# Where the last dots of the modulation weights run in a hybrid attention and convolution layer

## The chip, the cores and the metric

The kernel runs on one core of a Trainium2 chip. The metric is the device time of one execution in microseconds (us). The engines are TensorE (PE; PEld is its weight load), VectorE (DVE), ScalarE (ACT), GpSimd (POOL) and SyncE (SP), which issues all DMA transfers here from one queue in order.

## The reference

One layer over x (1024 tokens x 1024) with a context of 256 tokens. All six modulation vectors come from one product with `w_ada`; for the context the first two of them are needed.

```
sh1, sc1, gt1, sh2, sc2, gt2 = split(silu(c) @ w_ada + b_ada, 6)
csh1, csc1, ... = split(silu(c_ctx) @ w_ada + b_ada, 6)
hc = rmsnorm(ctx, g_pre_mix) * (1 + csc1) + csh1
kc, vc, gates_f, gates_b = parts of hc @ w_in         # gates: log_sigmoid(a @ w + b) / 16
s_f, s_b = final states of a gated linear attention over the context, both directions
hx = rmsnorm(x, g_pre_mix) * (1 + sc1) + sh1
p = hx @ w_in                                          # k, v, gates, q, og, sb, sc, sx
o = chunked gated linear attention from s_f and s_b, both directions, rmsnorm, * silu(og)
o_sc = sb * row_convolution(sc * sx)
x = x + gt1 * rmsnorm(concat(o, o_sc) @ w_out, g_post_mix)
x = x + gt2 * rmsnorm(conv_ffn(rmsnorm(x, g_pre_ffn) * (1 + sc2) + sh2), g_post_ffn)
```

## The kernel before

Products run on PE in three passes over values split in a high and a low part (`mm3`, whose lines L145 to L147 carry most of PE's records). Tokens go in tiles of 128: eight of x (`NT`) and two of the context (`NCT`).

The modulation vectors aren't made on PE. Of each 128 columns of `w_ada` a tile of 128x1024 floats (512 KB) is loaded, and DVE multiplies it by the broadcast silu(c) and sums along the row (L230, a "dot"). The first 16 are done early. The other 48 are drawn from one list by `some_ada(n)`: it first does the dots of all pending loads, then issues n new loads. In the text below they are numbered 0 to 47: loads 0 to 15 are of the context's shift and scale, 16 to 47 are columns 16 to 47, for gt1, sh2, sc2, gt2. Unless a place is given, a load goes by turns, `nada % 3`, into the pools `px` ("x"), `pgt` ("ada") and `px` again: loads with number 1, 4, ..., 19, 22, ..., 40, 43, 46 go to the one buffer of `ada`, the rest to `x`, which has eight buffers that `bc`, `gc`, `kw`, `kc`, `vc`, `hch`, `hcl`, `mraw`, `su` use as well. A load waits until its buffer has been read.

The stages around the change, in PE's order, which is the written one throughout:

- the q and token-major steps of x and the context. `token_major(2, tk)` for eight tiles of x, with loads 4 to 19; the context's keys `kc` for two tiles; `token_major(2, ...)` for the two tiles of the context; then `token_major(1, tk)` for eight tiles of x ("token steps", loads 20 to 37, three in the first two steps and two in the others), and for the two tiles of the context ("context steps", no loads).
- `gla()` and `stream()`, which take turns. `gla` first makes the gates: `ctx_decay(j)` for the two context tiles, then `decay(c)` for eight tiles c. Each is a product on PE (`gates_psum`, L486) into one of two banks, three steps on ACT (tile `ge`) and one on DVE (L495, result `gc` or `g`), which frees the bank. `ctx_keys` and `sums(c)` (L757: cumulative sums of g on PE, read by ACT into `bc`) follow one and two steps behind; `kx_prep` (L775 and L778 on DVE, an exponential on ACT) needs `bc`; `kx_turn` and `update` follow. `stream` is the rest of the input projection, 24 matrix products at a time for a half block, with the row convolution (L691 to L701 on DVE).
- In `gla` the ten last loads (38 to 47) are issued one a step, all into the buffer of `ada`, each done in the step behind it; `masks` (for the attention levels much later) are cast at c = 0 from `mraw`.

DVE, ACT and POOL keep the written order inside the token-major block, DVE also inside the first two steps of `gla` (`ORDERED`); there are two such blocks one behind the other, not tied to each other. Everything else on DVE, ACT, POOL and SP is put in order at build time by a planner from its own costs, with the program's order as priority; it may put an instruction ahead of others that are written earlier. So `row<-gv` (L1041, 1024 floats written to DRAM one by one, from gt1) is issued long before the place where it stands.

Of the kernel before, what the change touches and what calls it, by code (L numbers as in the profile page):

```python
# [8 lines left out]
F32 = mybir.dt.float32  # L9
# [12 lines left out]
P = 128  # L22
KT = D // P
NT = T // P
NCT = CT // P
H = 4
DK = 64
# [92 lines left out]
def build(nc, ap, out, dbg=None):  # L120
    V, S, G, PE, SY = nc.vector, nc.scalar, nc.gpsimd, nc.tensor, nc.sync
    names = iter(range(10**9))

    def nm(s="t"):
        return f"{s}{next(names)}"

    def act(o, i, fn=AF.Copy, **kw):
        return S.activation(o, i, fn, **kw)  # L128
# [13 lines left out]
    def mm3(ps, lhs, rhs, first, last, more=False):  # L142

        (lh, ll), (rh, rl) = lhs, rhs
        PE.matmul(ps, lh, rh, start=first, stop=False, skip_group_check=more)  # L145
        PE.matmul(ps, lh, rl, start=False, stop=False, skip_group_check=more)  # L146
        PE.matmul(ps, ll, rh, start=False, stop=last, skip_group_check=more)  # L147

    with tile.TileContext(nc) as tc, tc.manual_schedule(engines={mybir.EngineType.PE}):
        pools = {}  # L150

        def popen(name, side=None, **kw):
            cm = tc.tile_pool(name=name, side=side, **kw)
            pools[name] = (cm, cm.__enter__())
            return pools[name][1]
# [19 lines left out]
        def bank(n):  # L175
            return pools[n][1].tile([P, 512], F32, tag=n, name=nm("ps"))
# [30 lines left out]
        px = popen("px", "right", bufs=8)  # L207
        pgt = popen("pgt", "left", bufs=1)
# [12 lines left out]
        def ada_load(j, pool, tag, bufs):  # L221
            raw = pool.tile([P, D], F32, tag=tag, bufs=bufs, name=nm("ada"))
            SY.dma_start(raw, ap["ada"][j])
            return raw

        def ada_dot(j, which, raw, eng=None):

            dst = (gcol, gctx)[which][:, j : j + 1]
            if eng is None:
                V.tensor_tensor_reduce(raw, raw, cbs[which], 1.0, 0.0, ALU.mult, ALU.add, dst)  # L230
            else:
                eng.tensor_tensor(raw, raw, cbs[which], ALU.mult)
                act(raw, raw, AF.Copy, accum_out=dst)
# [265 lines left out]
        def ctx_load():  # L499
            for j in range(NCT):  # L500
                cxs.append(x_load(ap["ctx"], j))
                cdg.append(rms_diag(cxs[j]))
# [22 lines left out]
        def hc(kt, j):  # L525
            s = slice(j * P, (j + 1) * P)
            return hch[kt // 4][:, kt % 4, s], hcl[kt // 4][:, kt % 4, s]

        def token_major(g, tk, lhs, vv):
            pp = bank(ps_mm)  # L530
            for kt in range(KT):
                mm3(pp[:, :272], lhs(kt), (wah[g, kt], wal[g, kt]), kt == 0, kt == KT - 1)
            if g == 1:
                act(vv[:, :272], pp[:, :272])
                return
            al = cp.tile([P, 32], F32, tag="al", bufs=3, name=nm("al"))
            act(al, pp[:, 240:272])
            act(vv[:, 272:], pp[:, :240])
            als[tk] = al
# [9 lines left out]
        def xlhs(tk):  # L549
            s = slice(tk * P, (tk + 1) * P)  # L550
            return lambda kt: (hxh[kt][:, s], hxl[kt][:, s])
# [5 lines left out]
        def some_ada(n, where=None):  # L557

            for a, raw in pend:
                ada_dot(a[0], a[1], raw, a[2])  # L560
            pend.clear()
            for _ in range(n):
                a = next(adas, None)
                if a is not None:
                    where_ = where or ((px, "x", 8), (pgt, "ada", 1), (px, "x", 8))[nada[0] % 3]
                    pend.append((a, ada_load(a[0], *where_)))
                    nada[0] += 1

        als = {}
        with tc.manual_schedule(engines={mybir.EngineType.Activation, mybir.EngineType.DVE, mybir.EngineType.Pool}):  # L570
            ctx_load()
            some_ada(4)
            for hf in range(2):
                pq1 = bank(ps_mm)
                tsl = slice(hf * 512, hf * 512 + 512)
                for kt in range(KT):
                    mm3(pq1, wq1[kt], (hxh[kt][:, tsl], hxl[kt][:, tsl]), kt == 0, kt == KT - 1)
                act(qh[hf][:, 1, :], pq1, AF.Copy, scale=DK ** -0.5)
            for t in range(NT):
                vt[t] = pvo.tile([P, VW], F32, tag="vo", name=nm("v"))  # L580
            for tk in range(NT):
                some_ada(3 if tk < 3 else 2 if tk < 5 else 1)
                if tk == 3:
                    ada_affine_ctx(0)
                if tk == 5:
                    ada_affine_ctx(4)
                if 4 <= tk < 8:
                    ctx_lo()
                token_major(2, tk, xlhs(tk), vt[tk])
                if tk > 1:  # L590
                    put_aT(tk - 2)
                if 3 <= tk < 7:
                    ctx_lo = ctx_norm(tk - 3)
                if tk == NT - 1:
                    for kt in range(4):
                        wa_load(1, kt)
                        wa_split(1, kt)
            put_aT(NT - 2)
            kc = px.tile([P, NCT, QK], F32, tag="x", name="kc")
            vc = px.tile([P, NCT, VW], F32, tag="x", name="vc")  # L600
            for j in range(NCT):
                pp = bank(ps_mm)
                for kt in range(KT):
                    mm3(pp[:, :QK], hc(kt, j), (wah[0, kt][:, :QK], wal[0, kt][:, :QK]), kt == 0, kt == KT - 1)
                act(kc[:, j, :], pp[:, :QK])
            put_aT(NT - 1)
            for kt in range(4, KT):
                wa_load(1, kt)
            for j in range(NCT):
                token_major(2, NT + j, lambda kt: hc(kt, j), vc[:, j, :])  # L610
            for kt in range(4, KT):
                wa_split(1, kt)
            for tk in range(NT):
                some_ada(3 if tk < 2 else 2)
                token_major(1, tk, xlhs(tk), vt[tk])
                if 0 < tk <= NCT:
                    put_aT(NT + tk - 1)
            for j in range(NCT):
                token_major(1, NT + j, lambda kt: hc(kt, j), vc[:, j, :])
        pclose("pst")  # L620

# [1 line left out]
        pg_ = popen("pg", "right", bufs=1)  # L623
        tc.keep_in_program_order(S.preload_act_table_set("natural_log_exp_and_others"))
        masks = pg_.tile([P, 6, DK], U8, name="masks")
        mraw = px.tile([P, 6, DK], F32, tag="x", name="mraw")
        SY.dma_start(mraw, ap["masks"])
        og_d = [dr.tile([4, P, H, P], F32, name=f"ogd{c}") for c in range(2)]
        sc_d = [dr.tile([4, P, H, P], F32, name=f"scd{c}") for c in range(2)]
        x1_d = [dr.tile([P, D], F32, name=f"x1d{c}") for c in range(NT)]  # L630
# [103 lines left out]
        pe_ = popen("pe_", "right", bufs=1)  # L734
        flat = lambda t: t.rearrange("p f t -> p (f t)")

        def gla():
# [29 lines left out]
            def kx_prep(hf, d):  # L767
                e = (P - 1) if d == 0 else 0
                for hh in range(2):
                    act(decv[d * DK : d * DK + DK, hh, :, 4 * hf : 4 * hf + 4],  # L770
                        bc[hf][d][hh * DK : hh * DK + DK].rearrange("p f (c t) -> p f c t", t=P)[:, :, :, e],
                        AF.Exp, scale=ITAU)
                kx = pe_.tile([P, 2, 512], F32, tag="e", bufs=4, name=nm("kx"))
                b3 = bc[hf][d].rearrange("p f (c t) -> p (f c) t", t=P)
                V.tensor_tensor(kx.rearrange("p f (c t) -> p (f c) t", t=P),  # L775
                                b3[:, :, e : e + 1].broadcast_to([P, 8, P]), b3, ALU.subtract)
                act(kx, kx, AF.Exp, scale=ITAU)
                V.tensor_tensor(kx, kx, kh[hf], ALU.mult)  # L778
                kxs[hf, d] = kx
# [47 lines left out]
                V.tensor_copy(slot(NT - 1)[DK:P, :], s0[DK:P, :])  # L827

            slot = lambda c: su[c // 2][:, c % 2, :]
            for j in range(NCT):  # L830
                ctx_decay(j)
                some_ada(1, (pgt, "ada", 1))
                yield 1
            for c in range(NT):
                decay(c)
                if c == 0:
                    V.tensor_copy(masks, mraw)
                if 0 < c <= NCT:
                    ctx_keys(c - 1)
                if c > 1:  # L840
                    sums(c - 2)
                some_ada(1, (pgt, "ada", 1))
                if c == 4:
                    su = [px.tile([P, 2, 512], F32, tag="x", name=f"su{i}") for i in range(4)]
                    ctx_state()
                if c >= NT - 2:
                    kx_prep(0, c - NT + 2)
                yield 0.8 if c > 1 else 1
            some_ada(0)
            sums(NT - 2)  # L850
            yield 0.8
            sums(NT - 1)
# [818 lines left out]
```

## Time and profile before

| what | value |
|---|---|
| three runs | 1153.4, 1157.13 (median), 1157.71 us |
| the profiled execution | 1157.1 us |
| its span, first to last instruction | 1155.3 us |
| PE busy | 1120.4 us, 97% |
| DVE, ACT, POOL busy | 872.3, 528.9, 498.9 us |
| mean granted clock of TensorE | 0.993 |

Times in the profile count from the span's start. A timeline row gives start and duration, engine, line, operation, the tiles written and read, and in brackets how long the engine had been idle and what ended it. A waits row gives who waited for whom: total us, times, longest. The token and context steps of `token_major(1, ...)` run on PE from about 118 to 148 us, the steps of `gla` behind them.

### The profile page before, as it was taken

Reading aid. Unit: us, or ns where it says so; the run is one execution under the profiler, and the core shown is the slowest. Engines: PE = TensorE matmul, PEld = TensorE weight load, DVE = VectorE, ACT = ScalarE, POOL = GpSimd, SP = SyncE. Lnnn points to the kernel's source line nnn. Section 1 sums busy time; section 2 is a strip of 40 time slices with the busy share of each in tenths; the row PEclk is TensorE's granted clock in tenths of the full one; section 3 lists DMA queues with packets and bytes.
Section 4 is the critical chain, followed back from the end, with each engine's and each line's share of the span. In section 5 each row is a group of like instructions: output and inputs, shape, how many; then the busy total and the mean of one; then the engine's idle time right before and its main releaser. Section 6 shows DMA issues by size and latency. Waiting matters only on the chain. (4 is left out here: it accounts for less than half of the span.)

```text
span 1155.3 us, 16916 instructions
## 1 busy us (share of the span) xinstructions
PE 1120.4 (97%) x6272; PEld 927.1 (80%) x6272; DVE 872.3 (76%) x1182; ACT 528.9 (46%) x957; POOL 498.9 (43%) x467
## 2 busy tenths in 40 slices
PE   8899988999999999999999999999999999999997
PEld 6689977888887878887878788888887888888885
DVE  5876657899778556576888978787878787777676
ACT  6845156644344456655233242433333345544443
POOL 5211012347466111128777868687767780000002
PEclk9999999999999999999999999999999999999999
DMA  9884853522113283232343323232323169978572
GB/s 345 311 277 137 275 143 119 149 63 60 46 44 102 59 280 113 79 110 73 91 146 110 109 92 119 92 110 92 119 91 110 66 208 338 357 250 273 195 245 100
DMA packets 80132, 176.00 MB, mean 152 GB/s; under 512 B 9807, under 2 KB 21711, under 8 KB 80050
## 3 DMA queue, kind: packets, MB, share of 16 engines
q1 hardware_dynamic: 80050, 174.93, 45.9%
q8 instruction: 49, 0.80, 0.3%
q14 instruction: 33, 0.27, 0.1%
HBM read 142.12 MB, written 32.78 MB: 151 GB/s over the span
## 5 line engine op out<-in xcount | busy, mean ns | idle before, releaser
L1343 DVE SCALAR_TENSOR_TENSOR y<-u,cols,y 128x945 f32<-128x945 f32 (+2 forms) x176 | 214.8, 1222 | 3.7 <-ACT y L128 1.3
L145 PE MATMUL ps<-mx,p 128*128 128x512 f32 x440 | 174.3, 396 | 4.1 <-DVE g L1398 2.2
L146 PE MATMUL ps<-mx,p 128*128 128x512 f32 x440 | 173.1, 394 | 0.0
L147 PE MATMUL ps<-mx,p 128*128 128x512 f32 x440 | 173.1, 393 | 0.0
L135 POOL TENSOR_TENSOR p<-rs,p 128x512 fp32r<-128x512 f32 x88 | 115.3, 1314 | 88.3 <-ACT p L128 84.5
L643 POOL TENSOR_TENSOR wl<-wr,wh 128x256 fp32r<-128x256 f32 x64 | 62.0, 998 | 158.9 <-ACT wh L128 158.7
L147 PE MATMUL ps<-p,p 128*128 128x512 f32 x308 | 120.1, 390 | 0.2
L146 PE MATMUL ps<-p,p 128*128 128x512 f32 x308 | 120.0, 390 | 0.0
L145 PE MATMUL ps<-p,p 128*128 128x512 f32 x308 | 119.9, 389 | 0.0
L145 PE MATMUL ps<-hxh,wh 128*128 128x512 f32 x256 | 104.5, 408 | 1.2 <-DVE sc L701 1.2
L145 PEld LDWEIGHTS ps<-mx,p 128*128 128x128 f32 x440 | 83.1, 189 | 27.0 <-ACT u L128 5.7
L230 DVE CUSTOM_DVE_ANT_0 ada<-ada,cb 128x1024 f32<-128x1024 f32 x64 | 80.3, 1265 | 31.3 <-DMA ada<-in_ada 30.7
L146 PE MATMUL ps<-hxl,wh 128*128 128x512 f32 x256 | 100.6, 393 | 0.0
L147 PE MATMUL ps<-hxh,wl 128*128 128x512 f32 x256 | 100.5, 393 | 0.0
L128 ACT ACTIVATE p<-rs 128x512 fp32r<-128x512 f32 x88 | 54.5, 623 | 100.5 <-POOL rs L1193 100.5
L147 PEld LDWEIGHTS ps<-mx,p 128*128 128x128 f32 x440 | 83.1, 189 | 18.6
L146 PEld LDWEIGHTS ps<-mx,p 128*128 128x128 f32 x440 | 83.0, 189 | 18.1
L135 POOL TENSOR_TENSOR p<-wr,p 128x512 fp32r<-128x512 f32 x58 | 76.1, 1312 | 13.0 <-ACT p L128 13.0
L128 ACT ACTIVATE y<-u,cols 128x1024 f32<-128x1024 f32 x22 | 26.6, 1210 | 107.1 <-DVE u L1405 107.1
L145 PE MATMUL ps<-b,p 128*128 128x512 f32 x176 | 69.5, 395 | 0.0
L146 PE MATMUL ps<-b,p 128*128 128x512 f32 x176 | 69.4, 394 | 0.0
L147 PE MATMUL ps<-b,p 128*128 128x512 f32 x176 | 69.4, 394 | 0.0
(277 smaller groups left out, 2598.9 us busy)
## 6 DMA issues: line engine op xcount, KB each, us to landing
ada<-in_ada SPq DMA_DIRECT2D x64, 512.0 KB, 4.6
wr<-in_wu SPq DMA_DIRECT2D x48, 512.0 KB, 4.0
h<-hd SPq DMA_DIRECT2D x77, 256.0 KB, 4.5
hd<-h SPq DMA_DIRECT2D x73, 256.0 KB, 2.2
wdr<-in_wd SPq DMA_DIRECT2D x55, 256.0 KB, 3.7
wdr<-in_wd SPq DMA_DIRECT2D x22, 512.0 KB, 5.9
x<-in_x SPq DMA_DIRECT2D x16, 512.0 KB, 4.4
wr<-in_wb SPq DMA_DIRECT2D x16, 512.0 KB, 3.7
```

The source lines that it names most:

```text
L128: return S.activation(o, i, fn, **kw)
L135: (eng or V).tensor_tensor(lo, raw, hi.bitcast(F32), ALU.subtract)
L145: PE.matmul(ps, lh, rh, start=first, stop=False, skip_group_check=more)
L146: PE.matmul(ps, lh, rl, start=False, stop=False, skip_group_check=more)
L147: PE.matmul(ps, ll, rh, start=False, stop=last, skip_group_check=more)
L230: V.tensor_tensor_reduce(raw, raw, cbs[which], 1.0, 0.0, ALU.mult, ALU.add, dst)
L643: eng.tensor_tensor(lo[:, k : k + 2], raw[:, k : k + 2], hi[:, k : k + 2].bitcast(F32), ALU.subtract)
L1343: V.scalar_tensor_tensor(y3[:, ro, co], u3[:, ri, ci], col("wcf", 9 * p + 3 * (dr_ + 1) + dc + 1), y3[:, ro, co], ALU.mult, ALU.add)
```

## The change

- `some_ada(2)` is called in the first step of `kc` (dot 19, loads 20 and 21) and in each of the two context steps. Loads 22 to 39 are issued in the token steps, 40 to 43 in the context steps, and dots 38 to 41 are written in the context steps.
- In `gla` the calls with a place of their own go. There are three calls with two loads each or none left: at j = 1 (dots 42 and 43, loads 44 and 45), at c = 1 (dots 44 and 45, loads 46 and 47) and at c = 3 (dots 46 and 47). The loads take the places by turns.
- `mraw` takes a buffer of the pool `pe_` instead of `px` and is issued inside `gla`; the cast of `masks` stands at c = 2 instead of c = 0.
- `kx_prep(0, 0)` and `kx_prep(0, 1)` stand at c = 5 and 6 instead of 6 and 7.

```diff
             for j in range(NCT):
                 pp = bank(ps_mm)
+                if j == 0:
+                    some_ada(2)
                 for kt in range(KT):
@@
             for j in range(NCT):
+                some_ada(2)
                 token_major(1, NT + j, lambda kt: hc(kt, j), vc[:, j, :])
@@
         masks = pg_.tile([P, 6, DK], U8, name="masks")
-        mraw = px.tile([P, 6, DK], F32, tag="x", name="mraw")
-        SY.dma_start(mraw, ap["masks"])
@@
             slot = lambda c: su[c // 2][:, c % 2, :]
+            mraw = pe_.tile([P, 6, DK], F32, tag="e", bufs=4, name="mraw")
+            SY.dma_start(mraw, ap["masks"])
             for j in range(NCT):
                 ctx_decay(j)
-                some_ada(1, (pgt, "ada", 1))
+                if j:
+                    some_ada(2)
                 yield 1
             for c in range(NT):
                 decay(c)
-                if c == 0:
+                if c == 2:
                     V.tensor_copy(masks, mraw)
                 if 0 < c <= NCT:
                     ctx_keys(c - 1)
                 if c > 1:
                     sums(c - 2)
-                some_ada(1, (pgt, "ada", 1))
+                if c in (1, 3):
+                    some_ada(2)
                 if c == 4:
                     su = [px.tile([P, 2, 512], F32, tag="x", name=f"su{i}") for i in range(4)]
                     ctx_state()
-                if c >= NT - 2:
-                    kx_prep(0, c - NT + 2)
+                if c in (5, 6):
+                    kx_prep(0, c - 5)
                 yield 0.8 if c > 1 else 1
-            some_ada(0)
             sums(NT - 2)
```

## Rows read from the trace of the kernel before

**Rows 1.** The page's busy line of all engines: busy us, share of span, instructions.
```profile
PE 1120.4 (97%) x6272; PEld 927.1 (80%) x6272; DVE 872.3 (76%) x1182; ACT 528.9 (46%) x957; POOL 498.9 (43%) x467
```

**Rows 2.** Waits of PE, 148 to 232 us: us in total, times, longest.
```profile
PE ps L757 <- DVE g L495: 4.7, 2, 4.1
PE ps L486 <- DVE gc L495: 2.4, 1, 2.4
PE ps L486 <- DVE g L495: 1.7, 2, 1.4
PE ps L794 <- ACT kxt L128: 0.2, 1, 0.2
```

**Rows 3.** Timeline of PE, 154 to 200 us: its rows with idle time before them.
```profile
156.84 0.79 PE L486 MATMUL ps<-wgh,aT 98*128 98x512 f32 x1 [2.35 <-DVE gc L495]
...
168.63 0.50 PE L486 MATMUL ps<-wgh,aT 98*128 98x512 f32 x1 [0.31 <-DVE g L495]
...
174.19 0.50 PE L486 MATMUL ps<-wgh,aT 98*128 98x512 f32 x1 [1.38 <-DVE g L495]
...
189.70 1.13 PE L757 MATMUL ps<-tri,g 128*128 128x128 f32 x8 [0.66 <-DVE g L495]
...
197.64 2.00 PE L757 MATMUL ps<-tri,g 128*128 128x128 f32 x8 [4.08 <-DVE g L495]
```

**Rows 4.** Windows: length, busy us by engine, then PEclk, DMA share, GB/s.
```profile
156.70:160.10 3.40, 3.27 (x8) 2.59 (x9) 2.52 (x6) 2.44 (x5) 0.00 (x0) 0.50 0.00 0
...
197.70:201.10 3.40, 3.40 (x14) 3.25 (x15) 1.58 (x2) 1.39 (x6) 0.00 (x0) 0.50 0.75 294
```

**Rows 5.** Timeline of DVE, 151 to 168 us: dots 35 and 38, cast, first gate.
```profile
151.20 1.22 DVE L230 CUSTOM_DVE_ANT_0 ada<-ada,cb 128x1024 f32<-128x1024 f32 x1 [0.15 <-DMA ada<-in_ada]
...
155.82 0.36 DVE L837 CAST masks<-mraw 128x384 uint8<-128x384 f32 x1 [3.39 <-DMA mraw<-in_masks]
156.09 0.69 DVE L495 SCALAR_TENSOR_TENSOR gc<-ps,ge 128x512 f32<-128x512 f32 x1
...
166.73 1.23 DVE L230 CUSTOM_DVE_ANT_0 ada<-ada,cb 128x1024 f32<-128x1024 f32 x1 [5.49 <-DMA ada<-in_ada]
```

**Rows 6.** Timeline of ACT, 151 to 160 us: third step of the first gate.
```profile
152.91 0.73 ACT L128 ACTIVATE ge<-ge,small 128x512 f32<-128x512 f32 x1
```

**Rows 7.** Timeline of SP's queue, 150 to 154 us.
```profile
152.46 0.33 SPq L627 DMA_DIRECT2D mraw<-in_masks  x1
152.84 0.43 SPq L1041 DMA_DIRECT2D row<-gv  x1
```

**Rows 8.** Timeline of DVE, 182 to 198 us: two dots and the last gate.
```profile
182.05 1.23 DVE L230 CUSTOM_DVE_ANT_0 ada<-ada,cb 128x1024 f32<-128x1024 f32 x1 [2.17 <-DMA ada<-in_ada]
...
192.33 1.77 DVE L230 CUSTOM_DVE_ANT_0 ada<-ada,cb 128x1024 f32<-128x1024 f32 x1
...
196.81 0.68 DVE L495 SCALAR_TENSOR_TENSOR g<-ps,ge 128x512 f32<-128x512 f32 x1
```

**Rows 9.** Timeline of DVE, 118 to 146 us: weight splits, dots 20, 23, 32.
```profile
118.99 1.59 DVE L135 TENSOR_TENSOR wal<-war,wah 128x272 fp32r<-128x272 f32 x4 [5.83 <-ACT wah L128]
...
122.39 1.23 DVE L230 CUSTOM_DVE_ANT_0 ada<-ada,cb 128x1024 f32<-128x1024 f32 x1 [0.67 <-DMA ada<-in_ada]
...
128.63 1.23 DVE L230 CUSTOM_DVE_ANT_0 ada<-ada,cb 128x1024 f32<-128x1024 f32 x1 [0.65 <-DMA ada<-in_ada]
...
145.09 1.23 DVE L230 CUSTOM_DVE_ANT_0 ada<-ada,cb 128x1024 f32<-128x1024 f32 x1 [0.21 <-DMA ada<-in_ada]
```

**Rows 10.** The loads of ada issued from 117 to 153 us, time to landing.
```profile
DMA to landing us min/median/max: 3.6/4.3/5.5
```

**Rows 11.** Instructions on the tile kx: ns min/median/max, first and last start.
```profile
L775 DVE TENSOR_TENSOR kx<-bc x4: 1215/1220/1221, 189.5 to 203.7; 128x1024 f32<-128x1024 f32 x4
```

**Rows 12.** All 64 loads of ada in the span, time to landing.
```profile
DMA to landing us min/median/max: 3.3/4.6/9.6
```

**Rows 13.** DMA traffic from 155.7 to 162.3 us.
```profile
DMA packets 0, 0.00 MB, mean 0 GB/s; under 512 B 0, under 2 KB 0, under 8 KB 0
```

## The prediction, made before the change was run

> **What bounds the kernel now.** I read the page's busy line first: TensorE (PE) works 97% of the span, so 35 us of idle PE time and the time at a lowered clock are all that a reordering can win [rows 1]. Then the waits of PE alone, for 148 to 232 us, where the moved dots lie: all but 0.2 us of them end at a `logdecay` result (L495) on VectorE (DVE), in PE's `gates_psum` (L486, which needs the bank that an earlier L495 has read) or in `sums` (L757) [rows 2]. In order of time they are five: 2.35 us before 156.84, 0.31 before 168.63, 1.38 before 174.19, 0.66 before 189.70, 4.08 before 197.64 [rows 3]; together 8.78 us. Next the granted clock: 0.50 in 156.70 to 160.10 and in 197.70 to 201.10, right behind the two long idle times, at the level of 1.2 GHz instead of 2.4. PE was busy for 3.27 and 3.40 us in these, so half of that, 1.6 and 1.7 us, is what the clock took [rows 4]. The stretch thus holds 8.8 + 3.3 = 12.1 us.
>
> Why DVE was late is seen in its own order of time. Before 156.84 it finished dot 35 at 152.43 and stood 3.39 us until `mraw` landed, cast `masks` at 155.82, and only then did `gc` of context tile 0, whose input had been ready since ScalarE's third step ended at 153.64 [rows 5, 6]. `mraw` had been issued at 152.46, right behind dot 35, whose buffer it took [rows 7]. The 0.31 and 1.38 stand behind dots 38 and 39 waiting for their loads: dot 38 waited 5.49 us [rows 5]. The 4.08 is `decay(7)`, done on DVE only at 196.81; in the 15 us before it DVE ran three dots, of 1.23, 1.23 and 1.77 us (the first and the last are shown), the first after 2.17 us of waiting [rows 8].
>
> **The change, part by part.** No dot, load or other instruction is added or lost; only places and buffers change. Loads are numbered 0 to 47 as in the list above.
>
> *Loads 20 and 21 and dot 19 at the kc step.* Dot 19 takes 1.22 us of a stretch in which DVE stood idle for 5.83 us until 118.99, when the `wa` splits began [rows 9]. On SP the two loads pass the `wa` and `wr` loads that follow; what passes is two transfers, some 4.3 us each [rows 10] and one beside the other, of work whose first reader is that split. I cost this at nothing; without the idle time it would be 1.2 us of DVE, ahead of no PE work that waits.
>
> *The token steps.* Three buffers serve the loads: two of `x` and the one of `ada`, since `hch`, `hcl`, `kc` and `vc` hold the other six. Each load waits until the dot three back has freed its buffer, so the stretch is paced by landing plus dot: the loads landed in 3.6 to 5.5 us, median 4.3 [rows 10], and a dot takes 1.22. Before, dot 20 began at 122.39 [rows 9] and dot 35 at 151.20 [rows 5]: 15 dots in 28.8 us, 1.92 us each. The change does not add a buffer. Dots 20 and 21 now run at 120.5 and 121.8, behind the same weight splits (118.99 and 1.59 [rows 9]); load 22 has landed by then, load 23 goes out when dot 20 ends, 121.75, and dot 23 starts 4.3 later, at about 126.0. From there the pace holds.
>
> *The context steps.* Six loads and four dots more than before (dots 38 to 41) are now written ahead of `gc` of tile 0. Dot 41 starts at 126.0 + 18 x 1.92 = 160.6 at the mean pace and at 158.9 at 1.83 us, the pace of the evenest nine (dot 23 at 128.63, dot 32 at 145.09 [rows 9]); it ends 1.2 us later, and `gc`, 0.69, at 160.8 to 162.5. PE stands ready from 154.49 (156.84 less 2.35). So the first stall would not go with the mask cast: it would be 6.3 to 8.0 us instead of 2.35. The bound below is no stall, from `gc` being ready at 153.64. I take 161.0, a stall of 6.55 and so **+4.2 us**, near the lower of the paced values, because `hch` and `hcl` are read for the last time when the token steps end and some of the last loads may get their buffers. Behind that stall the clock falls as it did behind the shorter one; I take 1.7 for 1.6, **+0.1**. Queued behind dots 40 and 41 is all of DVE's first work on the gates, and PE waits for that.
>
> A rule that bears on this: the Trainium skill, "DMA: Bandwidth & Descriptors", section "Anatomy of one DMA", fits a transfer as 2.0 us plus its bytes over 436 GB/s, measured for DMAs issued by GpSimd. That would be 3.2 us for these 512 KB, a pace of 1.5 us and dot 41 ending near 153: no stall, as an estimate by that page. The rows, with 4.3 at the median, do not agree, and I go by them.
>
> *The mask cast.* `mraw` no longer waits for a dot's buffer; its place in SP's queue, with some loads ahead, decides when it lands. The 3.39 us wait is no longer what ends last before `gc`: the dots are. If the planner still puts the cast ahead of `gc`, it costs its 0.36 us, at most until a load issued beside it lands. Taken as nothing, with 1 us as the upper bound.
>
> *Dots 42 to 47, two loads ahead.* Instead of twelve dots in the `gla` steps there are six. The three dots in the 15 us ahead of `decay(7)` go: 1.23 + 1.23 + 1.77 us and 2.17 us of waiting, 6.4 us of DVE's queue, against a stall of 4.08 [rows 8, 3]. I take all of it, **-4.1**, with the clock behind it, **-1.7**, and the 1.38 before 174.19, **-1.4**. I leave 0.31 and 0.66 standing. Bounds: nothing more than 2 us is won if ScalarE's and DVE's `kx` work takes the place, and 8.1 if all four stalls go. The four dots behind 200 us go too, which is worth nothing: in the rest of the stretch PE is kept waiting for 0.2 us [rows 2].
>
> *`kx_prep` one step sooner.* The same instructions, but those of the second direction now stand ahead of `decay(7)`. DVE's two `kx` steps, 1.22 us the first [rows 11] and the second, of the same size, alike, take 2.4 us for one direction; that is less than the 6.4 us freed. Taken as nothing; if they fall just ahead of `decay(7)` up to 2.4 us of the 4.1 come back.
>
> *The sum:* +4.2 + 0.1 - 4.1 - 1.7 - 1.4 = -2.9 us against the profiled execution's 1157.1 us (its span is 1155.3, 1.8 us lie around it; the median of the runs is 1157.13): 1154.2. PE is the bound for the rest, so what is won by 230 us is kept.
>
> **The rivals.** By 0.5%, about what a measurement of this kernel can tell from no change, the bounds are 1151.3 and 1162.9.
>
> *The dots slip behind `gc`.* The two written blocks are not tied to each other, so the planner may place `gc` of tile 0 ahead of dots 40 and 41 if it thinks those loads late. Then the first stall is 2.4 to 4.4 us, as before or a little more, and the rest is won: 1157.1 - 7.2 + 0.6 = 1150.5 (1149 to 1152). For it: the cast was put ahead of `gc` in just this way [rows 5]. Against: the cast came early, so the planner takes loads to be quick, and then the dots come first.
>
> *The loads keep up.* The shortest landing of any load is 3.3 us [rows 12]. If all were so, the pace would be (3.3 + 1.2) / 3 = 1.5 us and dot 41, at 125.05 + 18 x 1.5 = 152.1, would end before `gc` is ready; the stall and its clock loss vanish: 1157.1 - 7.2 - 2.35 - 1.6 = 1145.9. Against it: the pace over 15 dots was 1.92. The page cited above would have it this way.
>
> *The slow row write.* Before, `row<-gv`, 1024 elements of 4 bytes, stood in SP's queue behind `mraw` [rows 7]. Issued at 152.84, it left the DMA engines without a packet from 155.7 to 162.3 [rows 13], and load 38, issued behind it, landed only at 166.7 [rows 5]. If the planner puts that write ahead of load 41, dot 41 and all PE work behind `gc` come up to 9.6 us later (152.84 to about 162.4): 1163.8, slower. It decides from that one place in SP's order; behind load 41 it delays only loads 46 and 47, which have some microseconds.
>
> **How the numbers follow.** Forecast 0.50 (1150 to 1158), dots behind `gc` 0.25, loads keep up 0.13, row write 0.12. The range is to leave out some 0.2: from 1147.0, short of most of the third case, to 1160.0, short of the fourth, and it takes in the bounds of the first stall (from as before to 8.0 us). Faster by over 0.5%: 0.05 of the forecast, 0.15 of the second, all 0.13 of the third: 0.33. Slower: the 0.12. The same: 0.55.
>
> **What would show it.** Right: before the third L486 behind the token steps, PE idle for 5 to 8 us, DVE there in dots that wait for loads, the cast no longer in the way; then no idle of over 1.5 us before 200 us, and one lowered clock instead of two. Wrong, to the faster side: `gc` on DVE right at 154 to 155. Wrong, to the slower: `row<-gv` in SP's queue among loads 38 to 41, or the idle of 4 us before `sums(7)` still there with `kx` in its place.

## The result, and the profile after

The changed kernel took 1159.34 us (median of 22 runs, 1157.03 to 1163.63), the kernel before 1157.72 on the same chip (22 runs): a ratio of means of 1.0019, 95% interval 1.0011 to 1.0028. The time is inside the forecast range and within 0.5%, but on the other side: some 2 us slower, where 2.9 us less were forecast. The profiled execution of the changed kernel took 1158.04 us, with a span of 1155.9. One of the 22 runs of the kernel before took 1379.23 us and is left out of the ratio.

The page's busy line hardly differs [rows 1]:

```profile
PE 1118.3 (97%) x6272; PEld 924.6 (80%) x6272; DVE 870.2 (75%) x1182; ACT 529.0 (46%) x957; POOL 493.0 (43%) x467
```

The waits of PE in the same stretch, 148 to 232 us (total, times, longest), to be held against [rows 2]:

```profile
PE ps L486 <- DVE gc L495: 9.0, 1, 9.0
PE ps L758 <- DVE g L495: 2.3, 1, 2.3
PE ps L486 <- DVE g L495: 0.4, 1, 0.4
PE ps L758 <- ACT kw L128: 0.3, 1, 0.3
```

and in order of time, PE's rows with idle time before them (against [rows 3]):

```profile
162.91 0.79 PE L486 MATMUL ps<-wgh,aT 98*128 98x512 f32 x1 [9.03 <-DVE gc L495]
...
175.61 1.16 PE L758 MATMUL ps<-tri,g 128*128 128x128 f32 x8 [0.35 <-ACT kw L128]
...
179.89 0.50 PE L486 MATMUL ps<-wgh,aT 98*128 98x512 f32 x1 [0.35 <-DVE g L495]
...
200.67 1.13 PE L758 MATMUL ps<-tri,g 128*128 128x128 f32 x8 [2.26 <-DVE g L495]
```

One wait grew from 2.35 to 9.03 us, the last fell only from 4.08 to 2.26, and the three short ones (2.35 in sum) became two of 0.35. The sum went from 8.78 to 11.99 us. The granted clock fell behind the same two waits as before [rows 4]; windows of these two stretches (length, busy us by engine, PEclk, DMA share, GB/s):

```profile
157.39:167.63 10.24, 4.72 (x11) 3.75 (x12) 6.20 (x13) 2.45 (x4) 0.00 (x0) 0.50 0.81 270
...
201.77:205.18 3.41, 3.41 (x12) 2.84 (x11) 2.41 (x3) 3.19 (x10) 0.00 (x0) 0.50 0.59 174
```

Half of PE's busy time in each is what 1.2 GHz instead of 2.4 took: 2.36 and 1.70 us, where it was 1.6 and 1.7. The stretch so holds 11.99 + 4.06 = 16.05 us that could be won, and held 12.1 before: 4.0 more.

Why the first wait is 9 us is in DVE's own order of time (its timeline, dots 23, 24 and 41 and the first gate):

```profile
124.67 1.23 DVE L230 CUSTOM_DVE_ANT_0 ada<-ada,cb 128x1024 f32<-128x1024 f32 x1 [1.30 <-DMA ada<-in_ada]
...
127.23 1.23 DVE L230 CUSTOM_DVE_ANT_0 ada<-ada,cb 128x1024 f32<-128x1024 f32 x1 [0.92 <-DMA ada<-in_ada]
...
161.02 1.22 DVE L230 CUSTOM_DVE_ANT_0 ada<-ada,cb 128x1024 f32<-128x1024 f32 x1 [1.55 <-DMA ada<-in_ada]
...
162.17 0.69 DVE L495 SCALAR_TENSOR_TENSOR gc<-ps,ge 128x512 f32<-128x512 f32 x1
```

From dot 23 to dot 41 it is 18 dots in 36.35 us, 2.02 each, with a dot of 1.23: DVE stands waiting for loads, and `gc` follows dot 41 at once. The masks' cast, 2.35 us of wait before, no longer appears in front of it. SP's queue has the row write behind load 45, as the forecast had it:

```profile
121.11 38.72 SPq L223 DMA_DIRECT2D ada<-in_ada  x21
159.94 0.37 SPq L832 DMA_DIRECT2D mraw<-in_masks  x1
160.36 0.90 SPq L223 DMA_DIRECT2D ada<-in_ada  x2
161.30 0.44 SPq L1045 DMA_DIRECT2D row<-gv  x1
```

And in front of the last `sums`, where three dots have gone [rows 8], DVE is busy all the same. First its timeline, then one row of ACT's and one of POOL's:

```profile
196.27 1.73 DVE L779 TENSOR_TENSOR kx<-kx,kh 128x1024 f32<-128x1024 f32 x1 [0.75 <-ACT kx L128]
197.93 1.21 DVE L696 SCALAR_TENSOR_TENSOR sc<-sc,cols,sc 128x504 f32<-128x504 f32 x1
199.18 0.74 DVE L697 SCALAR_TENSOR_TENSOR sc<-sc,cols,sc 128x504 f32<-128x504 f32 x1
199.84 0.68 DVE L495 SCALAR_TENSOR_TENSOR g<-ps,ge 128x512 f32<-128x512 f32 x1
```

```profile
197.61 0.73 ACT L128 ACTIVATE ge<-ge,small 128x512 f32<-128x512 f32 x1
```

```profile
194.60 4.00 POOL L644 TENSOR_TENSOR wl<-wr,wh 128x256 fp32r<-128x256 f32 x4 [17.53 <-ACT wh L128]
```

ACT's last step for the gate ended at 198.34; the gate ran 1.5 us later, behind a `kx` product and two steps of the row convolution that had been put ahead of it. Two of the three were long (1.73 and 1.21 us; elsewhere 1.22 and 0.74) while POOL split weights beside them. In the kernel before, that product and the second of these steps ran right behind the gate of 196.81 [rows 8]:

```profile
197.42 0.73 DVE L696 SCALAR_TENSOR_TENSOR sc<-sc,cols,sc 128x504 f32<-128x504 f32 x1
198.07 1.21 DVE L778 TENSOR_TENSOR kx<-kx,kh 128x1024 f32<-128x1024 f32 x1
```

There, too, ACT had a share in the wait. Its last step for that gate ended at 194.63, when PE had stood ready since 193.56 (197.64 less 4.08):

```profile
193.91 0.72 ACT L128 ACTIVATE ge<-ge,small 128x512 f32<-128x512 f32 x1
```

### The profile page after: what moved, and what is told of

Same layout as the page of the kernel before. It is cut to its first block, busy times and chain, and to the rows that moved or that the text cites. A ratio compares the mean times of both kernels' runs of the same rounds, so it can differ in the third digit from the quotient of the medians.

```text
span 1155.9 us, 16910 instructions
## 1 busy us (share of the span) xinstructions
PE 1118.3 (97%) x6272; PEld 924.6 (80%) x6272; DVE 870.2 (75%) x1182; ACT 529.0 (46%) x957; POOL 493.0 (43%) x467
## 5 line engine op out<-in xcount | busy, mean ns | idle before, releaser
L644 POOL TENSOR_TENSOR wl<-wr,wh 128x256 fp32r<-128x256 f32 x64 | 58.0, 939 | 168.1 <-ACT wh L128 168.0
```

The lines of the kernel that those rows point to most:

```text
L644: eng.tensor_tensor(lo[:, k : k + 2], raw[:, k : k + 2], hi[:, k : k + 2].bitcast(F32), ALU.subtract)
```

## The experiments

Ratios are to the kernel before on the same chip. The theory that all runs serve: the time is set by two places, the first gates behind dots that wait for their loads, and the last gates behind DVE work in front of them; in the changed kernel masks and `kx` count for nothing.

**The dots alone.** Of the change, only the ten dots; masks and `kx` as before.

```diff
+        mraw = px.tile([P, 6, DK], F32, tag="x", name="mraw")
+        SY.dma_start(mraw, ap["masks"])
...
-            mraw = pe_.tile([P, 6, DK], F32, tag="e", bufs=4, name="mraw")
-            SY.dma_start(mraw, ap["masks"])
...
-                if c == 2:
+                if c == 0:
                     V.tensor_copy(masks, mraw)
...
-                if c in (5, 6):
-                    kx_prep(0, c - 5)
+                if c >= NT - 2:
+                    kx_prep(0, c - NT + 2)
```

> The changed kernel with masks and kx as in the kernel before, so that only the ten dots are moved. Theory: the masks and kx parts are worth nothing beside the dots; the first gates wait 7 to 9 us, the cast of the masks is hidden in that wait, the wait before the last sums is about 2 us, and the time is that of the changed kernel, a ratio of 1.001 to 1.003. Rival: the masks part of the change does cost, as the run with it alone did (1.0040), because the masks' load is issued between the last loads of the weights; then this kernel is 2 us or more under the changed one, a ratio of 0.999 to 1.0005.

Measured: 1157.53 us, ratio 1.0018 (1.0010 to 1.0027), the changed kernel's own. PE's rows with idle time:

```profile
161.88 0.79 PE L486 MATMUL ps<-wgh,aT 98*128 98x512 f32 x1 [7.21 <-DVE gc L495]
...
180.47 0.49 PE L486 MATMUL ps<-wgh,aT 98*128 98x512 f32 x1 [1.61 <-DVE g L495]
...
201.02 1.62 PE L760 MATMUL ps<-tri,g 128*128 128x128 f32 x8 [2.01 <-DVE g L495]
```

So the dots are the change; the rest of it is not seen in the time. The 1.61 stands before the gates product that waits 0.35 in the changed kernel (at 179.89).

**`kx` back at its old steps.** The changed kernel with the last hunk undone.

```diff
-                if c in (5, 6):
-                    kx_prep(0, c - 5)
+                if c >= NT - 2:
+                    kx_prep(0, c - NT + 2)
```

> The changed kernel with the kx preparation back at its old two steps (c = 6 and 7), everything else kept. Theory: what little of the wait before the last sums was won (4.08 us before, 2.26 after) was won by the kx subtractions and one of their products standing ahead of the last gates' window; with them back, the wait before the last sums is 3.5 to 4.3 us and the time 1.5 to 2.5 us over the changed kernel's, a ratio to the kernel before of 1.003 to 1.005. Rival: the dots that left those steps won it and kx brought nothing; then the wait stays at 2.0 to 2.6 us and the ratio at 1.002. A third way: kx in its old place stands behind the last gates on VectorE, the wait is 0 to 1 us, and the step in the change was a loss; ratio 0.999 to 1.001.

Measured: 1158.75 us, ratio 1.0016 (1.0003 to 1.0028). The theory named there fell, its first rival holds: the wait before the last `sums` is 2.01 us, not 3.5 to 4.3. On DVE a `kx` product and the same two convolution steps stand directly ahead of the last gate whichever of the two places the program gives `kx`; what was won there came with the dots' leaving. The first wait was 7.00 us in this run.

**The masks alone.** The kernel before with only the masks part.

```diff
-        mraw = px.tile([P, 6, DK], F32, tag="x", name="mraw")
-        SY.dma_start(mraw, ap["masks"])
...
+            mraw = pe_.tile([P, 6, DK], F32, tag="e", bufs=4, name="mraw")
+            SY.dma_start(mraw, ap["masks"])
...
-                if c == 0:
+                if c == 2:
                     V.tensor_copy(masks, mraw)
```

> The kernel before with the mask part of the change alone (mraw in a buffer of pe_, issued inside gla; the cast written at c = 2). The planner still puts the cast ahead of gc of context tile 0 on DVE, and on SP mraw now stands behind the 4-byte row write. Theory (places in the queues decide, not places in the program): mraw lands some 9.6 + 3.3 us after 152.5, so PE idles about 11 us before the third gates product instead of 2.35, with a longer stretch at the lower clock: about 1168 us. Rival (the cast at c = 2 is out of the way): idle and lowered clock gone, about 1154 us.

Measured: 1160.93 us, ratio 1.0040 (1.0027 to 1.0053). The mechanism is as expected, the size smaller. SP's queue, then DVE:

```profile
152.24 0.43 SPq L1041 DMA_DIRECT2D row<-gv  x1
152.77 0.81 SPq L829 DMA_DIRECT2D mraw<-in_masks  x1
```

```profile
161.98 0.36 DVE L837 CAST masks<-mraw 128x384 uint8<-128x384 f32 x1 [7.65 <-DMA mraw<-in_masks]
162.25 0.69 DVE L495 SCALAR_TENSOR_TENSOR gc<-ps,ge 128x512 f32<-128x512 f32 x1
```

Although written two token tiles later, the cast is still put ahead of the first gate, and its load now stands behind the row write: it landed some 9 us after its issue, and PE waited 8.77 us.

**The masks alone, with the cast held in its place.** As before, but the cast can't be put ahead of what is written earlier.

```diff
-                if c == 0:
-                    V.tensor_copy(masks, mraw)
+                if c == 2:
+                    tc.keep_in_program_order(V.tensor_copy(masks, mraw))
```

> The kernel before with the mask part, the cast tied behind what is written before it on DVE at c = 2. Theory: gc of tile 0 runs when its input is ready, the 2.35 us idle and the lowered clock behind it go, and PE keeps that: about 1157.7 - 3.9 = 1153.8 us. Rival (DVE is the bound behind it, so the idle of 4.08 us before the last sums grows by as much): 1157 us or more.

Measured: 1154.45 us, ratio 0.9986 (0.9975 to 0.9997). The first wait is gone (0.19), but another of 3.10 us came before the sixth gates product (168.69), which needs the bank that the fourth gate reads, with a lowered clock behind it (169.88 to 173.29), so less was won than expected. The 4.08 us before the last `sums` stayed as they were, against the rival. Dot 38 stood in front of that fourth gate:

```profile
166.23 1.79 DVE L230 CUSTOM_DVE_ANT_0 ada<-ada,cb 128x1024 f32<-128x1024 f32 x1 [7.03 <-DMA ada<-in_ada]
```

**The same, with the row writes moved.** Both `row<-gv` writes issued at the half's turn in `gla`, and held there.

```diff
+                    gv_rows.extend((rows(16, "gp1"), rows(40, "gp2")))
...
-            SY.dma_start(d.rearrange("f p -> p f"), row_scale(gt0, gname))
+            tc.keep_in_program_order(SY.dma_start(d.rearrange("f p -> p f"), v))
...
-        SY.dma_start(gv1, rows(16, "gp1"))
-        gv2_row = rows(40, "gp2")
+        SY.dma_start(gv1, gv_rows[0])
+        gv2_row = gv_rows[1]
```

> The kernel before with the masks part and the cast tied behind its place (as in the run where only that was done), and the two scattered row writes of the scales moved on the queue to a stage in which no load of the weights is awaited. Theory: the row write of 1024 single 4-byte elements per transfer holds the queue for about 7 us, and it is why dot 38 waited 1.79 us for its load and the third gates 3.10 us; with it away both waits fall under 0.8 us, the lowered clock behind them goes, and the time is 2.5 to 4.5 us less than in that run: ratio 0.995 to 0.997. Rival: the loads are late anyway, from their three buffers; the wait shrinks by less than 1 us, ratio 0.998 to 0.999.

Measured: 1151.38 us, ratio 0.9949 (0.9933 to 0.9966); 0.37% less than without it. Dot 38 waits 1.51 us instead of 7.03 (the 1.79 in the expectation is not its wait but the time that it ran), and PE's wait of 3.10 us is gone:

```profile
160.19 1.23 DVE L230 CUSTOM_DVE_ANT_0 ada<-ada,cb 128x1024 f32<-128x1024 f32 x1 [1.51 <-DMA ada<-in_ada]
```

Counted from its own issue, load 38 reached its dot in 3.6 us (156.57 to 160.19), and in the run without this move in 8.5 (157.76 to 166.23). So the row write is what made the load behind it late, as the forecast's rival had taken from [rows 13], by some 5 us.

**The late dots behind the first gates.** The changed kernel without the two calls at the context steps; the dots go to the steps of `gla`, two at a time, and the cast is held.

```diff
             for j in range(NCT):
-                some_ada(2)
                 token_major(1, NT + j, lambda kt: hc(kt, j), vc[:, j, :])
...
-                if j:
-                    some_ada(2)
+                some_ada(2)
...
-                if c in (1, 3):
+                if c in (1, 2, 4):
                     some_ada(2)
```

> The changed kernel without the calls in the two context steps; instead gla calls for two loads at j = 0 and 1 and c = 1 and 2, with the last dots at c = 4; the cast is tied behind what is written before it on DVE. So dots 38 to 41 stand behind gc of tile 0. Theory (these four dots, waiting for their loads, are the idle time of 9.03 us): idle of at most 1 us there, no lowered clock behind it, about 1159.3 - 8.3 - 2.4 = 1148.6 us. Rival (the loads are late for whoever comes next): PE idles at the fourth gates product, 5 us or more, and the time stays within 2 us of 1158.

Measured: 1154.7 us, ratio 0.9996 (0.9979 to 1.0012). The 9 us are gone, but PE waits at the next gates:

```profile
155.50 0.50 PE L486 MATMUL ps<-wgh,aT 98*128 98x512 f32 x1 [0.74 <-DVE gc L495]
...
160.79 0.50 PE L486 MATMUL ps<-wgh,aT 98*128 98x512 f32 x1 [2.06 <-DVE gc L495]
...
170.15 0.50 PE L486 MATMUL ps<-wgh,aT 98*128 98x512 f32 x1 [4.82 <-DVE g L495]
```

The 4.82 stand behind dot 41, which waited 5.96 us for a load that had the row write of 155.73 ahead of it. The place of the dots made the 9 us, as the theory has it, but a place alone doesn't make the loads come sooner: the ratio stayed near 1, as the rival puts it.

**A fourth buffer.** The changed kernel, with one buffer more for loads 20 to 39, paid for with two of the six for `war`.

```diff
-            wars[g, kt] = pst.tile([P, 272], F32, tag="waraw", bufs=6, name=nm("war"))
+            wars[g, kt] = pst.tile([P, 272], F32, tag="waraw", bufs=4, name=nm("war"))
...
-                    where_ = where or ((px, "x", 8), (pgt, "ada", 1), (px, "x", 8))[nada[0] % 3]
+                    three = (px, "x", 8), (pgt, "ada", 1), (px, "x", 8)
+                    four = (*three, (pst, "ada4", 1))
+                    where_ = four[nada[0] % 4] if 20 <= nada[0] < 40 else three[nada[0] % 3]
```

> The changed kernel with a fourth buffer for loads 20 to 39 (in a pool that closes behind the token steps; a pool of weight rows gives up two of six buffers for the room). Theory (three buffers pace the loads, landing plus dot over three): pace from dot 23 on about 1.5 us instead of 1.97, dot 41 ends at 153 to 156, idle at most 2.5 us instead of 9.03, about 1150 us. Rival (the transfers are limited by what the DMA engines move, whatever the buffers): pace stays above 1.85, idle 7 to 9 us, about 1159 us.

Measured: 1152.99 us, ratio 0.9969 (0.9956 to 0.9981). DVE's dots 24 and 41, and PE's first wait:

```profile
125.31 1.23 DVE L230 CUSTOM_DVE_ANT_0 ada<-ada,cb 128x1024 f32<-128x1024 f32 x1 [0.39 <-DMA ada<-in_ada]
...
155.34 1.23 DVE L230 CUSTOM_DVE_ANT_0 ada<-ada,cb 128x1024 f32<-128x1024 f32 x1
```

```profile
157.24 0.50 PE L486 MATMUL ps<-wgh,aT 98*128 98x512 f32 x1 [2.88 <-DVE gc L495]
```

From dot 24 to dot 41 it is 17 dots in 30.03 us, 1.77 each; in the changed kernel 33.79 us, 1.99. Dot 24 itself is 1.9 us earlier, since one load more is ahead. The wait fell by 6.15 us. The pace hangs on the buffers, as the forecast had said, though four don't bring it to the 1.5 expected, so the rival has a share: the loads of this stretch took 5.2 us at the median with four in flight, 4.6 with three.

**The last gates first.** The changed kernel with `decay` at high priority.

```diff
-                decay(c)
+                with tc.high_priority():
+                    decay(c)
```

> The changed kernel with the gates of each token tile written at high priority, so that on VectorE the last gates stand ahead of the two state steps that preceded them in the changed kernel. Theory: the 2.26 us before the last sums are VectorE work in front of the last gates (two state steps of 1.2 us); with those behind, the wait before the last sums is 0 to 0.8 us, TensorE's lowered clock behind it (3.41 us long) is gone, and the lead at the end of the stage grows by 3 to 4 us; ratio 0.998 to 0.9995. Rival: the state steps that now stand behind the gates are wanted soon after, the wait goes there, and the ratio stays at 1.001 to 1.003. The 9 us wait of the first gates stays in either.

Measured: 1156.03 us, ratio 0.9989 (0.9978 to 0.9999), 0.3% under the changed kernel's. DVE's timeline, PE's and ACT's row, and a window from behind the first lowered clock to 232 us:

```profile
196.63 1.23 DVE L779 TENSOR_TENSOR kx<-kx,kh 128x1024 f32<-128x1024 f32 x1 [1.27 <-ACT kx L128]
197.77 0.68 DVE L495 SCALAR_TENSOR_TENSOR g<-ps,ge 128x512 f32<-128x512 f32 x1
198.37 0.73 DVE L696 SCALAR_TENSOR_TENSOR sc<-sc,cols,sc 128x504 f32<-128x504 f32 x1
199.14 0.74 DVE L697 SCALAR_TENSOR_TENSOR sc<-sc,cols,sc 128x504 f32<-128x504 f32 x1
```

```profile
198.60 1.13 PE L758 MATMUL ps<-tri,g 128*128 128x128 f32 x8 [0.36 <-DVE g L495]
```

```profile
196.49 0.72 ACT L128 ACTIVATE ge<-ge,small 128x512 f32<-128x512 f32 x1
```

```profile
167.00:232.00 65.00, 63.19 (x360) 54.07 (x359) 43.98 (x75) 45.30 (x94) 16.22 (x20) 1.00 0.40 87
```

The 2.26 us became 0.36, no lowered clock follows, and PE doesn't wait for the two convolution steps that now run behind the gate. The theory holds, with one addition: the priority moved ACT's steps as well. The last of them ended at 197.21 instead of 198.34, since the second no longer stood behind an exponential of `kx` and a step of the convolution; the gate ran 0.56 us behind it instead of 1.5. The first wait was 8.43 us here.

**All repairs, without and with the gates' priority.** Dots as in the run behind the first gates, the cast held, the fourth buffer for loads 20 to 37, the row writes moved; then `decay` at high priority as well.

```diff
-                    where_ = where or ((px, "x", 8), (pgt, "ada", 1), (px, "x", 8))[nada[0] % 3]
+                    three = (px, "x", 8), (pgt, "ada", 1), (px, "x", 8)
+                    four = (*three, (pst, "ada4", 1))
+                    where_ = four[nada[0] % 4] if 20 <= nada[0] < 38 else three[nada[0] % 3]
```

> All repairs together but the gates' priority: two dots each at context steps 0 and 1 and at token steps 1, 2 and 4, the cast tied, a fourth buffer for loads 20 to 37, the row writes moved. Theory: waits at the first gates as in the run with all repairs (under 2 us in sum), and about 2 to 2.5 us before the last sums with 3.41 us of lowered clock behind it, since the state steps stand ahead of the last gates again; 3 to 4 us over the run with all repairs, ratio 0.992 to 0.994. Rival: the gates' priority brought its gain at other places; the wait before the last sums is under 1 us here too, and the ratio 0.990.

> All repairs together: the two context calls left out, two dots each at context steps 0 and 1 of the gates and at token steps 1, 2 and 4, the cast tied to its place, a fourth buffer for loads 20 to 37, the row writes moved off the loads' stage, the gates at high priority. Theory: the waits of the first, second and third gates (0.74, 2.06 and 4.82 us without the buffer and with the row write in place) fall to 2 us in all, the wait before the last sums under 0.8 us, and at most one stretch of lowered clock is left in the stage; the time is 6 to 10 us under the kernel before, ratio 0.991 to 0.995. Rival: what is gained in this stage is given back where the loops of the stages behind wait for other things (the lead at 200 us is larger than at 876 us by 3 us or more); ratio 0.996 to 0.999.

Measured: 1148.98 us without the priority, ratio 0.9941 (0.9927 to 0.9955), and 1145.59 with it, ratio 0.9897 (0.9880 to 0.9914). Without it PE waits 2.52 us before the last `sums`, as expected, though the clock stayed at 1.00 behind that wait. The priority was worth 0.44%, some 5 us where 3 to 4 were expected; a wait of 1.33 us at the `sums` before the last is gone with it too. Of the 4.8 us between the two profiles' spans, 2.5 arise from 154 to 226 us; 1.1 were there before this stage, and 1.1 arise where only the run without the priority shows a lowered clock (at 528 us), so not all of the 5 us is shown to be the priority's. With it, the waits of PE in 148 to 232 us and the window over the same:

```profile
PE ps L773 <- ACT kw L128: 1.4, 1, 1.4
PE ps L486 <- DVE gc L495: 0.7, 2, 0.3
PE ps L773 <- ACT bc L128: 0.6, 1, 0.6
```

```profile
148.00:232.00 84.00, 81.33 (x501) 68.83 (x500) 62.06 (x108) 59.11 (x114) 21.48 (x24) 1.00 0.50 115
```

Of 16.05 us in waits and clock 2.7 are left, and the gain is a little more than was expected. It is kept to the end: a product that PE began at 876.13 us in the kernel before begins at 863.13, and of these 13.0 us of lead 10.9 are there at 226 us (1.0 already ahead of the stage). This version beats both kernels by 1%.

## Why the prediction was off

The terms of the forecast's sum, each against the traces:

| term | forecast, us | measured, us | from |
|---|---|---|---|
| first stall | +4.2 | +6.7 | 9.03 - 2.35 |
| clock behind it | +0.1 | +0.8 | 2.36 - 1.6 |
| stall before the last `sums` | -4.1 | -1.8 | 2.26 - 4.08 |
| clock behind it | -1.7 | 0 | 1.70 - 1.7 |
| the three short ones | -1.4 | -1.65 | 0.70 - 2.35 |
| sum | -2.9 | +4.0 | |

Of the +4.0, 0.6 cost nothing, since PE came to the first stall 0.6 us sooner than before (162.91 - 9.03 = 153.88, against 154.49). What is left, 3.4, is somewhat more than the later start that PE shows behind this stretch (the same product of `v` and `kxt` begins at 225.96 us, before at 223.33: 2.6 later); the rest is not placed. The spans of the two profiles differ by only 0.6 us, less than the medians, mainly since the execution of before had one more stretch of lowered clock later on (the last section).

*The step that failed* is "I take all of it", of the wait before the last `sums`: with the clock behind it, four of the seven us between forecast and sum. It put the whole 4.08 us down to DVE's queue. But ACT gave the gate its input only at 194.63, and from the gate's start to PE's it took another 0.83 us (196.81 to 197.64). With nothing ahead of the gate on DVE, PE would still have waited from 193.56 to about 195.5: an estimated 1.9 us of the 4.08 were not the queue's, and 2.2 were. In the changed kernel the two shares are 0.8 and 1.5. The dots did leave, but DVE's queue ahead of `decay(7)` didn't empty; the `kx` product and the convolution step that had run behind the gate were put in their place, and the `kx` product and the first convolution step were stretched beside POOL's splits. The bound was written down ("nothing more than 2 us is won if ScalarE's and DVE's `kx` work takes the place"), with the wrong end taken. A wait of 4.08 behind a queue of 6.4 us isn't won by taking the 6.4 away, unless the gate stands first in what is left; the run with the gates first shows that it was order, on ACT as well as on DVE. The clock went with it: a shorter wait still had a lowered clock behind it. That part is not certain to come, since waits of 2.25 and 2.52 us in other runs had none behind them (the last section).

*The first stall* was foreseen in place and cause, and mis-sized. I took 6.55 us from 6.3 to 8.0, near the pace of the evenest nine dots, 1.83 us, counting on buffers that come free at the end; the pace was 2.02, above even the mean of before, 1.92. Some buffers did come free: loads 41 and 42 were issued at 154.24 and 154.72, right behind load 40 (153.82). But load 41 reached its dot only 6.8 us after its issue, where 4.6 is the median landing of the stretch, so the early issue won nothing. The four profiles with this stage in the change's form show 9.03, 8.43, 7.21 and 7.00, 7.9 in the mean: the term is +5.6 rather than +4.2, with 1 us either way among these four kernels, each profiled once. The run with a fourth buffer shows that it was the pace. The estimate by the Trainium skill's page "DMA: Bandwidth & Descriptors" (section "Anatomy of one DMA"), a pace of 1.5 us and no stall, is not borne out: 1.99 with three buffers and 1.77 with four.

*Right were* the cast out of the way of the first gate, at no cost; the loads at the kc step for nothing; the row write behind load 45, so that it hurt only the loads behind it (dot 46 waited 2.23 us, at a place where PE waited 0.35); the short stalls smaller (though 0.97 and 1.61 us stand at one of them with `kx` back and with the dots alone); `kx` worth nothing in the time. Of the forecast's own signs three failed: the first wait was over 8 us, an idle of 2.26 us stood before the last `sums`, and two lowered clocks were left. Of the rivals, neither the slip of `gc` ahead of the dots nor quick loads nor the row write among loads 38 to 41 came about in the changed kernel.

## What to carry to other kernels

When work leaves a queue in front of a critical instruction, don't count the freed time: ask what moves up in its place, and whether anything puts the critical instruction first (here the removal brought 1.8 us of the wait; the order, on two engines, 1.9 more and the lowered clock of 1.7). And look first when its input is ready: that part of the wait no queue gives back. Work that waits for loads belongs behind the instruction that the bound engine waits for, and its pace comes from landing time plus use, shared among the buffers: a load written earlier comes no sooner if its buffer doesn't. Look in a queue for the transfer of many single elements, and move it to where nothing behind it is awaited.

## What the runs showed of the hardware

*Many single elements.* The row write of 1024 elements of 4 bytes held up what stood behind it on SP's queue in every run where it stood among loads: 9 us to land 192 KB of masks in the run of the masks alone, and 8.5 us from the issue of load 38 to its dot, 3.6 with the write away. The 6.6 us without a packet in the kernel before [rows 13] are not all its doing. In the first 3.4 no load was issued, since the buffer of load 38 came free only when dot 37 had ended; SP's next row after the write is

```profile
159.09 9.23 SPq L223 DMA_DIRECT2D ada<-in_ada  x2
```

whose first load is number 38. It landed 7.6 us later, where the median of the stretch ahead is 4.3 [rows 10]. So the 9.6 us that the forecast allowed this rival, counted from the write's own issue, are more than the runs show for what stands behind it: 4.9 us for load 38, and some 6 for the masks (9.2 us from issue to cast, 3.4 in the kernel before).

*The clock behind a wait of 2 us is not certain.* In the loops further on PE waits for `g` once, 2.0 to 2.2 us in all twelve profiles; behind it the clock was lowered in seven of them and not in five. Before, then after the change, PE's row and a window:

```profile
535.39 0.57 PE L145 MATMUL ps<-mx,p 128*128 128x512 f32 x1 [2.17 <-DVE g L1398]
```

```profile
535.61:539.02 3.41, 3.41 (x9) 2.63 (x9) 0.83 (x2) 0.00 (x0) 3.33 (x4) 0.50 0.59 179
```

```profile
537.96 0.47 PE L145 MATMUL ps<-mx,p 128*128 128x512 f32 x1 [2.17 <-DVE g L1402]
```

```profile
535.00:560.00 25.00, 22.83 (x99) 18.25 (x98) 15.59 (x17) 9.58 (x16) 24.78 (x20) 1.00 0.26 85
```

The same wait cost an estimated 1.7 us more, half of the 3.41, in one execution than in the other. In the gates' stage, too, 1.77 and 2.01 us had it behind them and 2.25 and 2.52 had not. Behind the waits of 7.0 to 9.0 us it lay lower for 6.8 or 10.2 us, a part of it still inside the wait.

*DVE beside POOL.* While POOL split `wl` from 194.60 on in the changed kernel, DVE's `kx` product took 1.73 us and the convolution step 1.21; in the gates-first run POOL's last split ended at 198.45, and the steps of 198.37 and 199.14 took 0.73 and 0.74. Which of the two is slowed goes, in these rows, by which began first. The `kx` product of the changed kernel began at 196.27, inside a split of POOL's (196.17, 0.75 us). That of the gates-first run began at 196.63, ahead of POOL's last split (196.71), and took 1.23, while the split took 1.74 instead of the 0.73 and 0.74 of the two ahead of it. The `sc<-sc,ps` step (194.84 in the changed kernel) and the gate (197.77 in the gates-first run), with one operand in PSUM, were not slowed beside a split (0.68 each). That agrees with the Trainium skill, "SBUF — State Buffer", section "Who interferes with whom": a VectorE instruction with two inputs in SBUF contends with a GpSimd instruction that reads SBUF, one with at most one such input, outside the two-port modes, doesn't.
